# x and the first adaLN weights requested at once, small vectors by GpSimd, the first adaLN chain ahead of the casts, half of the spilt x written later

## The chip, the core and the metric

One core of a Trainium2 chip runs the whole kernel. The metric is device time in microseconds. Engines are named as in the profile: PE (TensorE), DVE (VectorE), ACT (ScalarE), POOL (GpSimd) and SP (SyncE, which here only issues DMAs). SP's transfers run on queue q1, POOL's on queue q0; the same 16 DMA engines serve both.

## The reference

One layer of a conditioned decoder trunk, for 256 prompt tokens and 8 x 8 sample tokens (320 rows in all) that share the weights. Only the start matters here:

```python
mod = jax.nn.silu(c) @ w_ada + b_ada                 # 9 conditioning rows, 2048 -> 6 x 2048
sh1, sc1, g1, sh2, sc2, g2 = jnp.split(mod, 6, axis=-1)
h = _rmsnorm(x, norm1_g) * (1 + sc1) + sh1
p = h @ w_in                                         # 2048 -> 11280: q, k, v, og, u, ga, gb, alr
...                                                  # linear attention, pooling, w_o, SwiGLU FFN
x = x + g1 * (merged @ w_o)                          # x is needed again here
```

## The kernel before

Activations lie transposed: 16 k-tiles of 128 channels x 320 tokens. Every projection splits weight and activation into a high and a low part and runs three matmuls for each pair of tiles (`mm3`, lines 171 to 173: `hh`x`whi`, `hl`x`whi`, `hh`x`wlo`). A weight chunk is loaded by SP into one of three `raw` buffers (line 149); ACT makes `whi` (line 157) and DVE makes `wlo` (line 158). The raw buffer is free for the next request once both have read it.

An adaLN block of 256 output channels is `hada`: `hada_load` fetches 2 MB of `w_ada` in two DMAs of 1 MB (lines 223 to 225; two `araw` buffers), 32 small matmuls use them (line 236), ACT copies the result out of PSUM (line 239), PE transposes it, and DVE reduces it, adds the bias and for section 1 folds in `norm1_g` (lines 244 to 249). Sections 0 and 1 (shift and scale) of the first two k-tiles are needed before any projection can start.

The head (lines 423 to 471) loads c, the small vectors and x. c lands in rows of `junk`, is transposed on PE (16 transposes, line 435), goes through silu into `scT`, and is then overwritten: `junk` also takes the output of the squares that give each row's norm (line 462). `h_pre(k)` (line 476) transposes x into `xT`, scales it with `rx` into `xh` and writes `xT` to a scratch in HBM (`xspill`, by POOL, line 484); the `w_o` stage reads it back. `h_post(k)` applies scale and shift (`affine`, lines 342 to 344) and splits the result into `hh[k]` and `hl[k]` (lines 337 and 338).

The projections of group 0 run in six slices of the contraction, `SLICES = ((0, 2), (2, 4), (4, 6), (6, 8), (8, 12), (12, 16))`. Each slice goes through seven units: q, k, u (256 columns each, one half unit) and v, og, ga, gb (512 columns each). Between units the adaLN blocks and `h_pre`/`h_post` of the next slice are emitted. The framework orders the instructions of each engine by a simulated timeline; `tc.high_priority` moves code ahead, `tc.issue_after(x)` holds an instruction behind another one of its engine. After slice 6 the kernel goes on with groups 1 to 3, `w_o`, and the FFN.

Of the kernel before, what the change touches and what calls it, by code (L numbers as in the profile page):

```python
# [79 lines left out]
def body(tc, A):  # L80
# [71 lines left out]
    def split(raw):  # L152
        n = raw.shape[2]
        hi = wp.tile([P, 512 // n, n], F32R, tag="whi", bufs=WB, name=nm("whi"))
        lo = wp.tile([P, 512 // n, n], F32R, tag="wlo", bufs=WB, name=nm("wlo"))
        hi, lo = hi[:, 0:raw.shape[1]], lo[:, 0:raw.shape[1]]
        S.copy(hi, raw)  # L157
        V.tensor_sub(lo, raw, hi.bitcast(F32))  # L158
        return hi, lo

# [59 lines left out]
    def hada_load(sec, b0, pool, eng):  # L220

        blk = sec * KT + b0
        t = pool.tile([P, KT, 2 * P], F32, tag="araw", bufs=2, name=nm("hraw"))
        for k in range(0, KT, 8):
            eng.dma_start(t[:, k:k + 8], wada[:, k:k + 8, blk * P:(blk + 2) * P])
        return t

    def hada(sec, b0, t, pool):
# [10 lines left out]
        S.copy(sb, ps[:, 0:w])  # L239
# [8 lines left out]
        if sec == 1:  # L248
            V.scalar_tensor_tensor(dst, dst, 1.0, N1G[:, b0:b0 + 2].unsqueeze(2).broadcast_to([P, 2, 9]),
                                   op0=ALU.add, op1=ALU.mult)  # L250

# [88 lines left out]
    def affine(x, a, b, kt):  # L340

        V.tensor_scalar(x[:, 0:TP], x[:, 0:TP], modp(a, kt), modp(b, kt), op0=ALU.mult, op1=ALU.add)
        V.tensor_tensor(s3(x[:, TP:T]), s3(x[:, TP:T]), mods(a, kt), op=ALU.mult)
        V.tensor_tensor(s3(x[:, TP:T]), s3(x[:, TP:T]), mods(b, kt), op=ALU.add)
# [78 lines left out]
    with tc.tile_pool(name="head", bufs=1) as xp:  # L423
        junk = xp.tile([P, D], F32, name="junk")
        crow = junk[0:9, :]
        nc.sync.dma_start(crow[0:1, :], A["c_prompt"])
        nc.sync.dma_start(crow[1:9, :], A["c_sample"])
# [13 lines left out]
        nc.sync.dma_start(vr0, A["b_ada"].rearrange("o (r p) -> (o r) p", p=P))  # L441
        vr1 = xp.tile([4 * KT + 4, P], F32, name="vr1")
        for j, n in enumerate(("norm1_g", "norm2_g", "final_norm_g", "pool_scale")):
            a = A[n] if n == "final_norm_g" else A[n][0]
            nc.sync.dma_start(vr1[16 * j:16 * j + 16, :], a.rearrange("(r p) -> r p", p=P))
        nc.sync.dma_start(vr1[64:68, :], A["gla_norm_g"][0].rearrange("(r p) -> r p", p=P))
        nc.sync.dma_start(xn[0], x2d[0:P])
        nc.sync.dma_start(xn[1], x2d[P:2 * P])
        nc.sync.dma_start(xn[2][0:TS], A["x_sample"].rearrange("b t d -> (b t) d"))
        raws = {(s, 0): hada_load(s, 0, xp, nc.sync) for s in (0, 1)}  # L450
# [9 lines left out]
        for i in range(3):  # L460
# [13 lines left out]
        spilt = []  # L474

        def h_pre(k):
# [3 lines left out]
            xT = xp.tile([P, T], F32, tag="xT", bufs=2, name=nm("xT"))  # L480
            xh = xhs[k] = xp.tile([P, T], F32, tag="xh", bufs=4, name=nm("xh"))
            S.copy(xT, pt[:, 0:T])
            V.tensor_tensor(xh, pt[:, 0:T], rx, op=ALU.mult)
            spilt.append(nc.gpsimd.dma_start(xspill[k], xT).ins)

        def h_post(k):
            xh = xhs.pop(k)
            affine(xh, 1, 0, k)
            hilo(hh[k], hl[k], xh)

# [21 lines left out]
        def h_rows(b):  # L512

            def load(s):
                raws[s, b] = hada_load(s, b, xp, nc.gpsimd)
# [6 lines left out]
        with tc.high_priority():  # L522
            h_rows(0)[4]()
        us = [u for u in units(0) if u[0] in "qku"] + [u for u in units(0) if u[0] not in "qku" and u[1] == 0]
        apool = [xp]
        for si, (k0, k1) in enumerate(SLICES):
            last = k1 == KT
            bg = [] if last else [f for b in range(*SLICES[si + 1], 2) for f in h_rows(b)]
            if last:
                with tc.issue_after(spilt[-1]):  # L530
# [7 lines left out]
            for ui, (kind, i, col) in enumerate(us):  # L538
# [607 lines left out]
```

## Time and profile before

| | us |
|---|---|
| median of 3 runs (1978.18 to 1979.74) | 1978.41 |
| the profiled execution | 1972.99 |
| its span in the profile | 1971.2 |
| PE busy in the span | 1924.5 |
| granted TensorE clock, mean share of full speed | 0.993 |

The span counts from the first instruction to the last; 1.8 us of the execution lie around it. The profiled execution is 5.4 us below the median of the timed runs. Times in the rows are from the start of the span.

### The profile page before, as it was taken

To read this page: it belongs to the slowest core of one execution; us is meant where nothing else is said; L and a number is where in the kernel's file an instruction comes from. 1 tells how busy PE (TensorE), PEld (TensorE's weight loads), DVE (VectorE), ACT (ScalarE), POOL (GpSimd) and SP (SyncE) were. 2 spreads that over 40 slices of the span, in tenths; PEclk is the share of its full clock that TensorE was granted. 3 is DMA by queue.
4 is the path that set the end of the run, shared out by engine and by line. 5 is a ranking of instruction groups with operands and counts; after the bars stand their busy time and mean duration, and the time that the engine had idled before them with its cause. 6 is when DMAs were issued, how large, how long until landed. Compare 5 with 4: busy or idle time off the path is not lost.

```text
span 1971.2 us, 34613 instructions
## 1 busy us (share of the span) xinstructions
PE 1924.5 (98%) x13808; PEld 1825.2 (93%) x13808; DVE 1007.0 (51%) x1935; ACT 826.9 (42%) x1485; POOL 207.3 (11%) x323
## 2 busy tenths in 40 slices
PE   5999999999999999999999999999999999999997
PEld 4889888988998899989989999999999999999997
DVE  3776454666355535665574444444444444444554
ACT  4433343544345433553354333333333434344443
POOL 2231131221121112111030000000000000000000
PEclk9999989999999999999999999999999999999998
DMA  9996647777875788579845555444545444444442
GB/s 349 354 354 237 203 150 264 219 230 251 256 223 188 247 268 272 183 249 321 269 153 158 186 188 182 145 150 144 156 145 155 150 150 150 150 151 144 149 139 98
DMA packets 287308, 400.60 MB, mean 203 GB/s; under 512 B 11953, under 2 KB 243921, under 8 KB 286809
## 3 DMA queue, kind: packets, MB, share of 16 engines
q1 hardware_dynamic: 250170, 261.81, 42.7%
q0 software_dynamic: 36976, 136.57, 19.5%
q8 instruction: 108, 1.77, 0.4%
q14 instruction: 54, 0.44, 0.1%
HBM read 373.90 MB, written 24.67 MB: 202 GB/s over the span
## 4 chain that ended last, share of the span: by engine, by line
PE 82%; DMA 3%; ACT 1%; DVE 0%; issue 0%; POOL 0%; ACTq 0%; DVEq 0%
PE ps L172 25%; PE ps L171 25%; PE ps L173 25%; PE pm L301 3%; PE pm L135 1%; DMA araw<-w_ada 1%; PE pm L786 1%; PE pm L807 1%; DMA raw<-w_o 1%; DMA S<-state_gla 1%; PE pm L752 1%; DMA o_gs<-S 0%; PE pm L782 0%; PE pm L591 0%; PE pm L741 0%; PE psy L171 0%
## 5 line engine op out<-in xcount | busy, mean ns | idle before, releaser
L158 DVE TENSOR_TENSOR wlo<-raw,whi 128x512 fp32r<-128x512 f32 x952 | 657.7, 694 | 792.4 <-ACT whi L157 779.9
L157 ACT CAST whi<-raw 128x512 fp32r<-128x512 f32 x952 | 587.8, 622 | 948.3 <-PE ps L172 830.1
L171 PE MATMUL ps<-hh,whi 128*128 128x320 f32 x1408 | 441.9, 314 | 6.1 <-ACT hh L337 2.6
L172 PE MATMUL ps<-hl,whi 128*128 128x320 f32 x1408 | 440.4, 313 | 0.0
L173 PE MATMUL ps<-hh,wlo 128*128 128x320 f32 x1408 | 437.4, 312 | 0.0
L172 PE MATMUL ps<-h2l,whi 128*128 128x320 f32 x1408 | 434.7, 309 | 0.0
L171 PE MATMUL ps<-h2h,whi 128*128 128x320 f32 x1408 | 434.7, 309 | 0.0
L173 PE MATMUL ps<-h2h,wlo 128*128 128x320 f32 x1408 | 434.2, 309 | 0.0
L171 PEld LDWEIGHTS ps<-hh,whi 128*128 128x128 f32 x1408 | 265.2, 188 | 19.7 <-issue 9.0
L172 PEld LDWEIGHTS ps<-hl,whi 128*128 128x128 f32 x1408 | 265.3, 188 | 10.4 <-issue 9.4
L173 PEld LDWEIGHTS ps<-hh,wlo 128*128 128x128 f32 x1408 | 264.7, 188 | 8.0 <-issue 5.3
L171 PEld LDWEIGHTS ps<-h2h,whi 128*128 128x128 f32 x1408 | 264.4, 188 | 3.4 <-ACT ah L337 3.4
L172 PEld LDWEIGHTS ps<-h2l,whi 128*128 128x128 f32 x1408 | 264.5, 188 | 0.1
L173 PEld LDWEIGHTS ps<-h2h,wlo 128*128 128x128 f32 x1408 | 264.5, 188 | 0.0
L171 PE MATMUL ps<-ah,whi 128*128 128x320 f32 x704 | 217.7, 309 | 0.0
L172 PE MATMUL ps<-al,whi 128*128 128x320 f32 x704 | 216.5, 308 | 0.0
L173 PE MATMUL ps<-ah,wlo 128*128 128x320 f32 x704 | 216.5, 308 | 0.0
L172 PEld LDWEIGHTS ps<-al,whi 128*128 128x128 f32 x704 | 132.0, 187 | 0.0
L171 PEld LDWEIGHTS ps<-ah,whi 128*128 128x128 f32 x704 | 131.9, 187 | 0.0
L173 PEld LDWEIGHTS ps<-ah,wlo 128*128 128x128 f32 x704 | 131.9, 187 | 0.0
L269 POOL DMA_DIRECT2D araw<-w_ada x64 | 55.1, 864 | 397.2 <-PE pm L301 385.9
L172 PE MATMUL ps<-ml,whi 128*128 128x320 f32 x256 | 79.3, 310 | 0.0
(282 smaller groups left out, 1634.2 us busy)
## 6 DMA issues: line engine op xcount, KB each, us to landing
raw<-w_gu SPq DMA_DIRECT2D x176, 512.0 KB, 3.5
raw<-w_in SPq DMA_DIRECT2D x170, 512.0 KB, 4.4
araw<-w_ada POOLq DMA_DIRECT2D x64, 1024.0 KB, 8.7
raw<-w_down SPq DMA_DIRECT2D x80, 512.0 KB, 3.5
hraw<-w_ada POOLq DMA_DIRECT2D x28, 1024.0 KB, 9.8
S<-state_gla POOLq DMA_DIRECT2D x16, 1024.0 KB, 8.3
o_gs<-S POOLq DMA_DIRECT2D x16, 1024.0 KB, 6.9
raw<-w_o SPq DMA_DIRECT2D x32, 512.0 KB, 6.2
```

Of the source, the lines that this page charges most:

```text
L135: PE.transpose(out, in_, ident[:k, :k])
L157: S.copy(hi, raw)
L158: V.tensor_sub(lo, raw, hi.bitcast(F32))
L171: PE.matmul(ps, lhsT=whi, rhs=xhi, start=start, stop=False)
L172: PE.matmul(ps, lhsT=whi, rhs=xlo, start=False, stop=False)
L173: last_mm[:] = [PE.matmul(ps, lhsT=wlo, rhs=xhi, start=False, stop=stop).ins]
L269: nc.gpsimd.dma_start(t[:, r:r + step], wada[:, k0 + r:k0 + r + step, col:col + nb * P])
L301: PE.matmul(ps[32 * j:32 * j + 32, 0:w], lhsT=scT[:, k0 + r + j, :], rhs=ada_raw[n][:, r + j, :], start=k0 == 0 and first, stop=k0 + nk == ...
L752: PE.matmul(pt, lhsT=E["kdn"][:, s, d * P:(d + 1) * P], rhs=E["vn"][:, s], start=s == 0, stop=s == 1)
L786: PE.matmul(pt[32 * j:32 * j + 32, :], lhsT=qeP[:, d, 4 * gg + j, :], rhs=E["S0", gg, d][:, j], start=False, stop=d == 0, tile_position=(0 ...
L807: PE.matmul(pt, lhsT=E["kpn"][:, j, d * P:(d + 1) * P], rhs=E["vp"][:, gg], start=True, stop=True)
```

## The change

- SP requests x first: the sample rows, then the two prompt tiles, then the four 1 MB pieces of `w_ada` for the first block of sections 0 and 1. For block 0 the upper half of the contraction (k-tiles 8 to 15), which the matmuls use first, is requested first.
- c, `b_ada` and the norm vectors are requested by POOL instead of SP; the identity matrix that the transposes need is made ahead of everything on POOL, and the zeroing of the unused rows of x moves from POOL to DVE.
- The first casts of weights (`whi` of q, k and u) may issue on ACT only after the copy of section 1's block; the first `wlo`, and the scaling of the next tiles, may issue on DVE only after `affine` of k-tile 0; `h_post(1)` follows it.
- POOL requests `w_ada` for the second block (`(s, b) == (0, 2)`) only after it has read the finished scale of block 0 (`anchor`). The matmuls of the second block are held behind the og unit of slice 1 (`first_mm`).
- For k below 8, `xT` lies in parts of the `merged` tiles that are not used yet, and its write to `xspill` is issued in the last slice, ahead of POOL's loads there.

```diff
-        S.copy(hi, raw)
-        V.tensor_sub(lo, raw, hi.bitcast(F32))
+        with tc.issue_after(first_casts[0]) if first_casts else nullcontext():
+            S.copy(hi, raw)
+        with tc.issue_after(first_casts[1]) if first_casts else nullcontext():
+            V.tensor_sub(lo, raw, hi.bitcast(F32))
...
-        for k in range(0, KT, 8):
+        for k in (8, 0) if b0 == 0 else (0, 8):
...
-        with tc.high_priority():
+        with tc.high_priority(), tc.issue_after(first_mm[0]) if first_mm else nullcontext():
...
+        with tc.high_priority():
+            make_identity(nc, ident)
+        nc.gpsimd.dma_start(crow[0:1, :], A["c_prompt"])
+        nc.gpsimd.dma_start(crow[1:9, :], A["c_sample"])
         xn = [xp.tile([P, D], F32, name="xn%d" % i) for i in range(3)]
-        G.memset(xn[2][TS:P], 0.0)
         x2d = A["x_prompt"][0]
+        nc.sync.dma_start(xn[2][0:TS], A["x_sample"].rearrange("b t d -> (b t) d"))
+        nc.sync.dma_start(xn[0], x2d[0:P])
+        nc.sync.dma_start(xn[1], x2d[P:2 * P])
+        raws = {(s, 0): hada_load(s, 0, xp, nc.sync) for s in (0, 1)}
         V.memset(scT, 0.0)
-        make_identity(nc, ident)
+        V.memset(xn[2][TS:P], 0.0)
...
-        for i in range(3):
+        for i in (2, 0, 1):
             n = P if i < 2 else TS
             S.activation(junk[:n], xn[i][:n], AF.Square, accum_out=ssq[:n, i:i + 1])
...
-            xT = xp.tile([P, T], F32, tag="xT", bufs=2, name=nm("xT"))
+            xT = merged[1 + k // 4 * 2][:, k % 4] if k < 8 else xp.tile([P, T], F32, tag="xT", bufs=2, name=nm("xT"))
             xh = xhs[k] = xp.tile([P, T], F32, tag="xh", bufs=4, name=nm("xh"))
             S.copy(xT, pt[:, 0:T])
-            V.tensor_tensor(xh, pt[:, 0:T], rx, op=ALU.mult)
-            spilt.append(nc.gpsimd.dma_start(xspill[k], xT).ins)
+            with tc.issue_after(first_casts[1]) if first_casts else nullcontext():
+                V.tensor_tensor(xh, pt[:, 0:T], rx, op=ALU.mult)
+            if k < 8:
+                parked.append((k, xT))
+            else:
+                spilt.append(nc.gpsimd.dma_start(xspill[k], xT).ins)
...
             def load(s):
-                raws[s, b] = hada_load(s, b, xp, nc.gpsimd)
+                with tc.issue_after(anchor(mod[:, KT, 0:1])) if (s, b) == (0, 2) else nullcontext():
+                    raws[s, b] = hada_load(s, b, xp, nc.gpsimd)
...
         with tc.high_priority():
-            h_rows(0)[4]()
+            evicted = hada(1, 0, raws.pop((1, 0)), xp)
+            first_casts += [evicted, h_post(0)]
+            with tc.issue_after(first_casts[1]):
+                h_post(1)
...
             if last:
+                with tc.issue_after(spilt[-1]):
+                    for k, xT in parked:
+                        nc.gpsimd.dma_start(xspill[k], xT)
...
+                if ui in (2, 4):
+                    first_mm[:] = last_mm if si == 0 else []
+                if ui == 2:
+                    first_casts.clear()
```

## Rows read from the trace of the kernel before

**Rows 1.** Windows: stretch, length, each engine's busy time (instructions), clock, DMA share, GB/s.

```profile
40.00:60.00 20.00, 20.00 (x182) 17.40 (x186) 11.85 (x31) 10.78 (x20) 4.68 (x6) 1.00 0.99 366
1000.00:1900.00 900.00, 899.34 (x6161) 886.44 (x6160) 423.82 (x711) 363.97 (x616) 20.09 (x40) 1.00 0.50 155
```

**Rows 2.** Timeline of PE: start, length, instruction, [idle before it <- what ended that].

```profile
3.86 1.84 PE L135 MATMUL pm<-cst,junk 9*128 9x9 f32 x16 [3.86 <-DMA junk<-c_sample]
...
24.84 1.93 PE L236 MATMUL pm<-hraw,scT 128*32 128x256 f32 x32 [0.42 <-DMA hraw<-w_ada]
28.62 0.44 PE L135 MATMUL pm<-cst,adasb 128*128 128x128 f32 x2 [1.84 <-ACT adasb L239]
...
32.27 0.90 PE L171 MATMUL ps<-hh,whi 128*128 128x320 f32 x2 [2.56 <-ACT hh L337]
...
35.93 1.93 PE L236 MATMUL pm<-hraw,scT 128*32 128x256 f32 x32
...
41.84 0.31 PE L171 MATMUL ps<-hh,whi 128*128 128x320 f32 x1
```

**Rows 3.** Timeline of SP's queue: when each request was issued.

```profile
0.74 0.35 SPq L426 DMA_DIRECT2D junk<-c_prompt  x1
...
4.08 0.35 SPq L447 DMA_DIRECT2D xn<-x_prompt  x1
...
5.58 11.27 SPq L225 DMA_DIRECT2D hraw<-w_ada  x4
...
27.31 1.38 SPq L149 DMA_DIRECT2D raw<-w_in  x2
```

**Rows 4.** Timeline of ACT in the head and the first units.

```profile
14.26 1.91 ACT L462 ACTIVATE junk<-xn 64x2048 f32<-64x2048 f32 x1 [0.40 <-DMA xn<-x_sample]
...
28.20 0.36 ACT L239 COPY adasb<-pm 128x256 f32<-128x256 f32 x1
...
31.76 0.82 ACT L337 CAST hh<-xh 128x320 fp32r<-128x320 f32 x2 [1.58 <-DVE xh L344]
35.95 0.62 ACT L157 CAST whi<-raw 128x512 fp32r<-128x512 f32 x1 [3.38 <-DMA raw<-w_in]
```

**Rows 5.** Timeline of DVE: scaling of x, first wlo, and the chain behind section 1.

```profile
22.09 0.89 DVE L483 TENSOR_TENSOR xh<-pm,rx 128x320 f32<-128x320 f32 x2
...
26.59 0.69 DVE L158 TENSOR_TENSOR wlo<-raw,whi 128x512 fp32r<-128x512 f32 x1 [1.68 <-ACT whi L157]
...
29.09 0.23 DVE L244 TENSOR_REDUCE mod<-pm 128x18 f32<-128x72 f32 x1
...
29.79 0.41 DVE L342 TENSOR_SCALAR xh<-xh,mod 128x256 f32<-128x256 f32 x1
```

**Rows 6.** Timeline of POOL: the requests for the second block's first section.

```profile
23.82 1.79 POOL L225 DMA_DIRECT2D hraw<-w_ada  x2 [1.82 <-PE pm L236]
```

**Rows 7.** Single raw requests, at 27.31, 29.05 and 170.27: KB, us to landing.

```profile
raw<-w_in SPq DMA_DIRECT2D x1, 512.0 KB, 8.6
...
raw<-w_in SPq DMA_DIRECT2D x1, 512.0 KB, 14.6
...
raw<-w_in SPq DMA_DIRECT2D x1, 512.0 KB, 3.6
```

**Rows 8.** PE's longest wait behind the head (timeline); windows around both long waits.

```profile
264.46 0.63 PE L171 MATMUL psy<-dh,whi 128*128 128x320 f32 x1 [2.42 <-ACT dh L337]
...
24.00:32.00 8.00, 3.45 (x42) 2.17 (x42) 5.15 (x16) 3.12 (x7) 4.55 (x6) 1.00 1.05 404
...
32.00:35.00 3.00, 2.73 (x10) 2.71 (x11) 0.89 (x2) 0.58 (x2) 0.00 (x0) 0.50 1.03 409
...
265.00:274.00 9.00, 7.67 (x27) 7.00 (x27) 2.64 (x6) 1.24 (x2) 2.37 (x6) 0.50 0.32 92
```

**Rows 9.** The last slice: POOL's first adaLN load (timeline), and its matmuls (one line's instructions).

```profile
149.12 1.80 POOL L269 DMA_DIRECT2D araw<-w_ada  x2 [2.63 <-DMA hraw<-w_ada]
...
L301 PE MATMUL pm<-araw,scT x128: 379/379/403, 209.6 to 246.7; 128*32 128x256 f32 x128
```

More of the change, by code (lines that the diff above doesn't have):

```diff
@@ L156, in split @@
         hi, lo = hi[:, 0:raw.shape[1]], lo[:, 0:raw.shape[1]]
-        S.copy(hi, raw)
-        V.tensor_sub(lo, raw, hi.bitcast(F32))
+        with tc.issue_after(first_casts[0]) if first_casts else nullcontext():
+            S.copy(hi, raw)
+        with tc.issue_after(first_casts[1]) if first_casts else nullcontext():
+            V.tensor_sub(lo, raw, hi.bitcast(F32))
         return hi, lo
+    first_casts = []
+    first_mm = []
     def split_chunk(src, nk, nn):
@@ L238, in hada @@
         sb = pool.tile([P, w], F32, tag="adasb", name=nm("adasb"))
-        S.copy(sb, ps[:, 0:w])
+        out = S.copy(sb, ps[:, 0:w]).ins
         pt = misc()
@@ L250, in hada @@
                                    op0=ALU.add, op1=ALU.mult)
+        return out
     PLAN = [(sec, b, 2, 16) for sec in (4, 2, 3) for b in range(0, KT, 2)] + [(5, 0, 4, 16), (5, 4, 4, 16), (5, 8, 4, 8), (5, 12, 4, 8)]
@@ L343, in affine @@
         V.tensor_tensor(s3(x[:, TP:T]), s3(x[:, TP:T]), mods(a, kt), op=ALU.mult)
-        V.tensor_tensor(s3(x[:, TP:T]), s3(x[:, TP:T]), mods(b, kt), op=ALU.add)
+        return V.tensor_tensor(s3(x[:, TP:T]), s3(x[:, TP:T]), mods(b, kt), op=ALU.add).ins
     xspill = dp.tile([KT, P, T], F32, name="xspill")
@@ L440, in body @@
         vr0 = xp.tile([6 * KT, P], F32, name="vr0")
-        nc.sync.dma_start(vr0, A["b_ada"].rearrange("o (r p) -> (o r) p", p=P))
+        nc.gpsimd.dma_start(vr0, A["b_ada"].rearrange("o (r p) -> (o r) p", p=P))
         vr1 = xp.tile([4 * KT + 4, P], F32, name="vr1")
@@ L444, in body @@
             a = A[n] if n == "final_norm_g" else A[n][0]
[L445 to L450, printed above, removed]
+            nc.gpsimd.dma_start(vr1[16 * j:16 * j + 16, :], a.rearrange("(r p) -> r p", p=P))
+        nc.gpsimd.dma_start(vr1[64:68, :], A["gla_norm_g"][0].rearrange("(r p) -> r p", p=P))
         pt = misc()
@@ L474, in body @@
         spilt = []
+        parked = []
         def h_pre(k):
@@ L479, in h_pre @@
                 tr(pt[:, i * P:(i + 1) * P], xn[i][:, k * P:(k + 1) * P])
-            xT = xp.tile([P, T], F32, tag="xT", bufs=2, name=nm("xT"))
+            xT = merged[1 + k // 4 * 2][:, k % 4] if k < 8 else xp.tile([P, T], F32, tag="xT", bufs=2, name=nm("xT"))
             xh = xhs[k] = xp.tile([P, T], F32, tag="xh", bufs=4, name=nm("xh"))
             S.copy(xT, pt[:, 0:T])
-            V.tensor_tensor(xh, pt[:, 0:T], rx, op=ALU.mult)
-            spilt.append(nc.gpsimd.dma_start(xspill[k], xT).ins)
+            with tc.issue_after(first_casts[1]) if first_casts else nullcontext():
[4 more added lines that the diff above has]
+                spilt.append(nc.gpsimd.dma_start(xspill[k], xT).ins)
         def h_post(k):
             xh = xhs.pop(k)
-            affine(xh, 1, 0, k)
+            done = affine(xh, 1, 0, k)
             hilo(hh[k], hl[k], xh)
+            return done
         def alr_proj(walr, cum):
```

2 lines of the change are left out of this document (removed).

## The prediction, made before the changed kernel ran

> **What bounds the kernel now.** I read the windows first. From 40 us on PE is busy without a gap, and so it is through the long stages [rows 1]. Whatever starts PE's dense work earlier therefore shortens the run by as much, unless PE later waits for what used to be in time. The timeline of PE shows where the dense work starts: the first projection matmul at 32.27, after a wait for `hh` [rows 2]. So the case is decided in the first 45 us, and I followed the chain that ends at 32.27 back through the timelines of PE, DVE, ACT and SP.
>
> The reader is to see three pieces. First, data: the last piece of `w_ada` for section 1 came at about 24.8, since PE stood ready and was released by that DMA [rows 2]. SP asked for x only at 4.08, behind seven small transfers, and for `w_ada` from 5.58 [rows 3]; between the two ends the queue simply works through its bytes. Second, the 32 matmuls of section 1, 1.93 us, ending at 26.77 [rows 2]. Third, 5.5 us from there to 32.27. That part is longer than its work: ACT was casting weights and copied the block only at 28.20, 1.43 us late [rows 4], and DVE put other tiles between the steps.
>
> **The request order.** SP's first request goes out at 0.74, its first for x at 4.08 [rows 3]. With the small ones gone, x goes out 3.34 us earlier, and all behind it on the same queue. I move the landing of the last piece from 24.8 to 21.5. The small vectors (about 150 KB) still need the same DMA engines; at the 366 GB/s of a busy stretch that is 0.4 us [rows 1], which the old order paid too.
>
> **The half order.** The upper half of each block is now first, and the matmuls use it first. In section 1 only 16 of 32 matmuls then stand behind the last landing: half of 1.93 is 0.97 us, a gain of 0.97. They end at 22.5.
>
> **The chain ahead of the casts.** Without foreign work I add its steps. Copy to transpose 0.42 (28.20 to 28.62), transpose to reduce 0.47 (to 29.09), reduce, bias and gain 0.70 (to 29.79), `affine` of one tile 0.8 (its first of three steps is 0.41, the others I estimate at half of that), cast of `hh` to first matmul 0.51 (31.76 to 32.27) and 0.1 for the first hand-over: 3.0 us [rows 2, 4, 5]. The first projection matmul so comes at 25.5, 6.8 us earlier than now: 3.3 from the requests, 1.0 from the half order, 2.5 from the chain.
>
> **What the wait of the casts costs.** The held `whi` casts are three of 0.62 us on ACT [rows 4]; they fit into the 2.6 us that the chain spends on PE and DVE behind the copy, so I take nothing. The held `wlo` is on the path of something else. Today the first `wlo` ends at 27.28, 5 us ahead of the first projection matmul, and frees a raw buffer; SP asks for v's weights at 27.31 [rows 3, 5]. After the change the first `wlo` runs only when `affine` of tile 0 is done, at about 25.0, and ends at 25.7. v's request thus moves 1.6 us earlier, while PE moves 6.8 us earlier. Queued behind it on DVE are `hl`, tile 1 and the next `wlo`; on SP the requests of og and ga.
>
> How long v then takes is the one large unknown. Three rows bound it: 8.6 us where POOL had its big loads out, 14.6 for the request two places behind, 3.6 with the engines free [rows 7]. At 25.7 POOL's first piece has been out for 1.3 us, against 3.5 us in the old case (23.82 to 27.31) [rows 3, 6], so the backlog is smaller but the competition is the same. I take 7.6, nearer to 8.6, and keep 5.8 to 8.6 for the forecast. v lands at 33.3, its cast takes 0.62 [rows 4], and v's matmuls start at 34.0.
>
> PE meanwhile has q, k and u: 36 matmuls. In the old run v started at 41.84, with one adaLN block (1.93) and its transposes (0.44) done in between [rows 2]; without these it is 39.5, so q, k and u took 7.2 us from 32.27. From 25.5 they end at 32.7. PE waits 1.3 us for v, where it used to have the second block as filler; that block is now held behind og, and its request by `anchor` until 24.3. **The sum** at this point is 39.5 less 34.0, 5.5 us earlier. og comes 0.3 us late by the same competition (its request waits for the second `wlo`): 5.2 us remain. With v at its bounds, landing 5.8 or 8.6 us after its request, they are 6.8 (PE then never waits) and 4.2.
>
> **The spill.** Eight writes of 160 KB, 1.3 MB, leave the first stages, worth some 3 us of DMA time there. No row before shows PE waiting for it, so I book no gain; it covers the idle stretch of the DMA engines between the first loads and POOL's held request. The eight requests now stand on POOL ahead of the last slice's loads: two of the larger ones took 1.79 us [rows 6], so eight take at most 7.2. The loads at 149.12 then issue up to 7 us later, and their matmuls start at 209.6 [rows 9]: a cover of 60 us. I take zero, up to 0.5 if q1's chunks are slowed for these 3 us.
>
> **Small moves.** The zeroing of x's unused rows took POOL 1.8 us; on DVE it lies in a stretch where DVE has nothing to do. c goes through POOL now. In the old run it was asked for at 0.74 and there at 3.86, and its transposes took 1.84 [rows 2, 3]. POOL makes the identity first and needs up to 0.9 us for each request [rows 6], so it has asked by about 3; I allow 4 us with x on the same engines, and c is there at 7. Since `junk` is reused, the squares wait for them. From the last square's start at 14.26 to scaled x at 22.09 it took 7.8 us [rows 4, 5]; three squares in a row add 4.2. Transposes, silu (0.3) and this put scaled x at about 21, 3 us before the scale of block 0 is. Zero cost.
>
> Here a rule speaks against the change. The Trainium skill (SBUF — State Buffer, "SBUF: two separate sides") says that a DMA issued by POOL has its descriptors written by GpSimd, which is locked out while VectorE runs a two-port operation, and advises SP or ACT instead. No run here shows such a lock. If the 1.9 us zeroing on DVE were such an operation, c would come at 9, still a us inside the cover, and the sum would not change.
>
> **The clock.** In the wait of 2.56 us before 32.27 the granted clock fell to half and stayed there past 35; after a wait of 2.42 us at 264 it was half until 274; the wait of 1.84 us before 28.62 left it whole [rows 2, 8]. Half is 1.2 GHz of 2.4. A fall of some 3.4 us costs 1.7 us of work, one of 10.2 us 5.1. My new wait before the first projection is about 2.0 us, and the one for v 1.3. If the clock holds at 25.5, q, k and u end sooner, and PE only waits longer for v, whose landing is fixed; so this changes the sum only when v is early. The Trainium skill (TensorE: Matmul & The Clock Gate, Part 1) adds that the monitor runs free of the kernel, so that the point of change shifts between runs; by that, either wait may fall on either side.
>
> **The rivals.**
>
> *No new wait.* v lands within 5.5 us and the clock holds at the start. For it: the queue is nearly empty when v is asked for. Against: 8.6 and 14.6 us in that stretch [rows 7]. Then 6.8 and half of the 1.7 us of half clock are kept: 7.6, or 1970.8.
>
> *Given back to the clock.* v lands 8.6 us after its request, PE waits 2.3 us, close to the 2.42 of the later fall, and the clock falls. For it: the row of v itself, and PE has lost its filler. With v at 8.6 the 4.2 us left lose 1.7 to 5.1 us: 1975.9 to 1979.3, no change to be seen.
>
> *Slower.* v is served like the third request of the old run, 14.6 us [rows 7], because POOL now puts four pieces out in one go ahead of it. Then v starts at 40.9, 1.4 us later than the old 39.5, plus a fall of 5.1: 6.5 us slower, 1985. With such a fall the change is slower than before once v takes over 8.6 us, and by 4 us once it takes over 11.7.
>
> *The head is bound elsewhere.* The change does not do what it says if c by POOL is late. c at 15 instead of 7 would put scaled x at 29 and the first projection at about 30.5: 1.8 us gained, no change to be seen. For it: the 14.6 us of a request in a full queue. Against it: c is only nine rows, and no more than x stands ahead.
>
> **How the numbers follow.** Forecast 52%, no new wait 14%, given back to the clock 19%, late c 5%, slower 10%. The profiled execution was 1972.99 for a span of 1971.2; the sum gives it 1967.8. Against the median of 1978.41 it is 1978.4 less 5.2, 1973.2; I carry the difference over, since nothing in the sum depends on where the 5.4 us between profile and median come from. A difference under 0.2%, 4 us, can't be told from none with this kernel. The forecast alone spans 1971.6 to 1974.2. The range reaches from the middle of the best rival, 1970.8, to the top of the clock's, 1979.3, and leaves out the slower case. Faster: forecast (less 4% in which the framework's new order loses a us elsewhere) and no new wait, 62%. Same: these 4, the clock and late c, 28%. Slower: 10%.
>
> **What would show it.** In the changed profile: SP's x requests at 0.7 to 2; section 1's last matmuls near 22; the copy right behind them; the first projection matmul at 25 to 26; v's `whi` cast released by its DMA at 32 to 34.5; no half clock after that; the loads of the last slice 5 us later without a wait for them. The forecast is wrong if the first projection matmul is not before 28, if PE waits over 2.4 us for v, or if waits show up in a stage that was dense before.

## The result and the profile after

The changed kernel is slower. Its median is 1984.3 us (1978.18 to 1991.05, 20 runs) against 1975.66 us (1970.51 to 1979.74, 20 runs) of the kernel before on the same chips: a ratio of 1.0046, 95% interval 1.0037 to 1.0056, or 9 us. The prediction was 5.2 us faster. (The three runs behind its 1978.41 are the three slowest of these 20.) The profiled execution took 1982.23 us, its span is 1980.1 us, its mean granted clock 0.994. (The new line numbers are up to 12 higher in the head and more behind it: `mm3` is now L176 to L178, the adaLN matmuls L241, `wlo` L160, `hl` L344.)

The windows of the changed kernel, with the columns of [rows 1]: stretch, length, busy time of PE, PEld, DVE, ACT and POOL, clock, DMA share, GB/s.

```profile
33.00:40.00 7.00, 4.70 (x17) 4.30 (x18) 3.48 (x8) 0.46 (x1) 2.93 (x4) 0.51 0.84 285
40.00:43.40 3.40, 1.31 (x9) 1.05 (x8) 0.91 (x2) 1.56 (x3) 0.00 (x0) 1.00 1.03 361
43.40:46.80 3.40, 3.17 (x12) 3.17 (x13) 0.38 (x1) 1.31 (x3) 0.00 (x0) 0.50 1.03 357
...
40.00:60.00 20.00, 17.68 (x132) 15.83 (x135) 7.69 (x13) 9.51 (x16) 1.75 (x2) 0.91 0.82 275
60.00:80.00 20.00, 16.77 (x170) 12.98 (x161) 11.94 (x30) 6.33 (x14) 3.51 (x4) 1.00 1.02 350
```

Between 40 and 60 us PE was busy for all of 20.00 us before [rows 1]; now it is 17.68, and 16.77 in the next 20 us. The clock is at half twice, for some 10.2 us together (before: once, for 3.4 us). PE's timeline shows where it waits; the last row is the counterpart of the long wait in [rows 8].

```profile
9.85 1.84 PE L135 MATMUL pm<-cst,junk 9*128 9x9 f32 x16 [9.85 <-DMA junk<-c_sample]
...
22.97 0.32 PE L135 MATMUL pm<-cst,vr 68*128 68x68 f32 x1
23.76 3.18 PE L241 MATMUL pm<-hraw,scT 128*32 128x256 f32 x32 [0.47 <-DVE rx L478]
...
27.71 1.93 PE L241 MATMUL pm<-hraw,scT 128*32 128x256 f32 x32
...
32.99 0.76 PE L176 MATMUL ps<-hh,whi 128*128 128x320 f32 x2 [1.47 <-ACT hh L343]
36.05 0.63 PE L177 MATMUL ps<-hl,whi 128*128 128x320 f32 x1 [2.30 <-DVE hl L344]
...
43.63 0.64 PE L176 MATMUL ps<-hh,whi 128*128 128x320 f32 x1 [2.32 <-ACT q L403]
...
69.27 1.93 PE L241 MATMUL pm<-hraw,scT 128*32 128x256 f32 x32 [2.73 <-DMA hraw<-w_ada]
...
274.76 0.42 PE L176 MATMUL psy<-dh,whi 128*128 128x320 f32 x1 [2.42 <-ACT dh L343]
```

At the last row the changed kernel is 10.3 us behind (274.76 against 264.46 [rows 8]). At the end of the span it is 8.9: the half clock behind that wait is 3.4 us long instead of 10.2, and small later waits take part of this back. So the loss lies where the gain was expected. It has these pieces: the first projection matmul comes at 32.99 instead of 25.5 as predicted, 0.7 us later than before; then PE waits 2.30 us for `hl`, 2.32 us for v and 2.73 us for a block of `w_ada`; and at the half clock PE is busy for 7.9 us (4.70 and 3.17 in the windows above), where before it was some 3.1 (2.73 in the 3 us of [rows 8], the rest just behind), 4.8 more, which costs half of that, 2.4. They sum to 10.5 us, close to the 10.3, though not exactly the same thing. The windows from the first projection matmul to the start of the long wait, before and then changed, give it in full:

```profile
32.27:262.04 229.77, 225.90 (x1852) 201.95 (x1852) 140.64 (x295) 86.23 (x166) 50.91 (x72) 0.99 0.82 290
32.99:272.34 239.35, 229.31 (x1852) 203.79 (x1852) 143.15 (x301) 86.21 (x166) 55.78 (x80) 0.98 0.86 289
```

Both have the same 1852 matmuls. PE is idle for 10.0 us instead of 3.9 and busy for 3.4 us more; with the later start that is 0.7 + 6.2 + 3.4 = 10.3. The three waits named are 7.35 of the 10.0; the smaller waits, which the first sum leaves out, were 1.2 us longer in the kernel before, and the busy time grew by 1.0 us more than the 2.4 worked out for the clock.

What released these waits stands in the timelines of the other engines, here in order of time.

```profile
1.31 0.65 POOL L434 DMA_DIRECT2D junk<-c_prompt  x1 [0.37 <-issue]
1.96 0.55 POOL L435 DMA_DIRECT2D junk<-c_sample  x1
...
2.47 13.14 SPq L230 DMA_DIRECT2D hraw<-w_ada  x4
...
30.00 0.37 ACT L244 COPY adasb<-pm 128x256 f32<-128x256 f32 x1 [2.61 <-PE pm L135]
...
32.35 3.58 POOL L230 DMA_DIRECT2D hraw<-w_ada  x4 [0.30 <-issue]
32.77 1.28 DVE L160 TENSOR_TENSOR wlo<-raw,whi 128x512 fp32r<-128x512 f32 x2
33.48 2.41 SPq L149 DMA_DIRECT2D raw<-w_in  x3
33.98 0.88 DVE L492 TENSOR_TENSOR xh<-pm,rx 128x320 f32<-128x320 f32 x2
34.78 0.68 DVE L160 TENSOR_TENSOR wlo<-raw,whi 128x512 fp32r<-128x512 f32 x1
...
35.51 1.10 DVE L344 TENSOR_TENSOR hl<-xh,hh 128x320 fp32r<-128x320 f32 x2
...
41.84 1.14 ACT L158 CAST whi<-raw 128x512 fp32r<-128x512 f32 x2 [5.76 <-DMA raw<-w_in]
...
56.50 1.75 POOL L230 DMA_DIRECT2D hraw<-w_ada  x2 [20.57 <-PE pm L241]
```

`w_ada` is asked for at 2.47 instead of 5.58 [rows 3], but its data are not much earlier. The head is the place to look at the DMA queues: from 14 to 24 us nothing but `w_ada` moves, in packets of 1 KB. First the kernel before, then the changed one (packets, MB, and the time of the packets as a share of 16 engines).

```profile
DMA packets 3819, 3.86 MB, mean 386 GB/s; under 512 B 49, under 2 KB 3819, under 8 KB 3819
...
q1 hardware_dynamic: 3819, 3.86, 108.7%
```

```profile
DMA packets 3468, 3.48 MB, mean 348 GB/s; under 512 B 69, under 2 KB 3468, under 8 KB 3468
...
q1 hardware_dynamic: 3468, 3.48, 109.1%
```

16 engines x 10 us x 1.087 / 3819 is 45.5 ns for a packet before, and 50.3 ns after; the median of the single packets is 46 and 51. The same transfer runs a tenth slower, with the engines as full in both. Nothing in the diff says that it should.

### The profile page after: what moved, and what is told of

Same layout as the page of the kernel before. It is cut to its first block, busy times and chain, and to the rows that moved or that the text cites. A ratio compares the mean times of both kernels' runs of the same rounds, so it can differ in the third digit from the quotient of the medians.

```text
span 1980.1 us, 34612 instructions
## 1 busy us (share of the span) xinstructions
PE 1926.2 (97%) x13808; PEld 1824.3 (92%) x13808; DVE 1008.0 (51%) x1936; ACT 826.1 (42%) x1485; POOL 212.4 (11%) x331
## 3 DMA queue, kind: packets, MB, share of 16 engines
q1 hardware_dynamic: 249904, 261.65, 42.5%
## 4 chain that ended last, share of the span: by engine, by line
PE 83%; DMA 1%; ACT 1%; POOL 0%; DVE 0%; issue 0%; ACTq 0%; DVEq 0%
PE ps L176 25%; PE ps L177 25%; PE ps L178 25%; PE pm L307 3%; PE pm L135 1%; PE pm L810 1%; PE pm L831 1%; PE pm L776 1%; DMA raw<-w_o 1%; DMA araw<-w_ada 1%; PE pm L765 0%; PE pm L806 0%; PE pm L706 0%; PE pm L615 0%; POOL w L890 0%; PE pm L787 0%
## 5 line engine op out<-in xcount | busy, mean ns | idle before, releaser
L160 DVE TENSOR_TENSOR wlo<-raw,whi 128x512 fp32r<-128x512 f32 x952 | 656.7, 693 | 788.1 <-ACT whi L158 775.6
L176 PE MATMUL ps<-hh,whi 128*128 128x320 f32 x1408 | 442.6, 315 | 6.2 <-ACT q L403 2.3
L178 PE MATMUL ps<-hh,wlo 128*128 128x320 f32 x1408 | 438.6, 313 | 0.1
L176 PE MATMUL ps<-h2h,whi 128*128 128x320 f32 x1408 | 434.6, 309 | 0.0
L178 PE MATMUL ps<-h2h,wlo 128*128 128x320 f32 x1408 | 434.1, 308 | 0.0
L176 PEld LDWEIGHTS ps<-hh,whi 128*128 128x128 f32 x1408 | 265.7, 189 | 21.4 <-issue 9.2
L178 PEld LDWEIGHTS ps<-hh,wlo 128*128 128x128 f32 x1408 | 265.5, 189 | 8.2 <-issue 5.3
L176 PEld LDWEIGHTS ps<-h2h,whi 128*128 128x128 f32 x1408 | 264.3, 188 | 3.4 <-ACT ah L343 3.4
L178 PEld LDWEIGHTS ps<-h2h,wlo 128*128 128x128 f32 x1408 | 264.4, 188 | 0.0
L176 PE MATMUL ps<-ah,whi 128*128 128x320 f32 x704 | 217.7, 309 | 0.0
L178 PE MATMUL ps<-ah,wlo 128*128 128x320 f32 x704 | 216.5, 308 | 0.0
L176 PEld LDWEIGHTS ps<-ah,whi 128*128 128x128 f32 x704 | 131.9, 187 | 0.0
L178 PEld LDWEIGHTS ps<-ah,wlo 128*128 128x128 f32 x704 | 131.9, 187 | 0.0
```

The lines of the kernel that those rows point to most:

```text
L176: PE.matmul(ps, lhsT=whi, rhs=xhi, start=start, stop=False)
L178: last_mm[:] = [PE.matmul(ps, lhsT=wlo, rhs=xhi, start=False, stop=stop).ins]
```

## The experiments

The traces gave three suspects on the engines' queues (theory A): c by POOL comes late; the held `wlo`, once released, goes ahead of `hl` on DVE and delays v's request; the second block, held behind og, no longer fills PE's wait for v and keeps its buffers until 56. The rival (theory B) was the slow packets. All timed comparisons are listed first (e0 and e8, single runs, stand in the text); "place" is where the `hraw` buffers begin in SBUF by the program's allocation, as the rest after division by 128.

| run | place | c late | wlo held | block held | ratio to before | interval |
|---|---|---|---|---|---|---|
| before | 0 | | | | 1 | |
| changed | 64 | x | x | x | 1.0046 | 1.0037 to 1.0056 |
| e1 | 64 | | x | x | 1.0028 | 1.0018 to 1.0039 |
| e2 | 64 | x | | x | 1.0021 | 1.0009 to 1.0033 |
| e3 | 64 | x | x | | 1.0011 | 1.0000 to 1.0022 |
| e7 | 64 | | | | 1.0014 | 1.0003 to 1.0025 |
| e6 (old half order) | 64 | x | x | x | 1.0051 | 1.0032 to 1.0071 |
| e9 (before, moved) | 64 | | | | 1.0026 | 1.0017 to 1.0036 |
| e10 | 0 | x | x | x | 1.0029 | 1.0016 to 1.0041 |
| e15 | 0 | x | x | | 0.9998 | 0.9987 to 1.0009 |
| e16 | 0 | | | x | 0.9991 | 0.9982 to 1.0000 |
| e11 | 0 | | | | 0.9998 | 0.9986 to 1.0009 |
| e12 (before, requests alone) | 0 | | | | 1.0002 | 0.9992 to 1.0013 |
| e4 (before, spill alone) | 0 | | | | 1.0002 | 0.9992 to 1.0011 |
| e13 (before, later buffers) | 0 | | | | 0.9990 | 0.9979 to 1.0001 |
| e14, e18 (e11, later buffers) | 0 | | | | 0.9982, 0.9984 | 0.9971 to 0.9994, 0.9974 to 0.9994 |
| e17 (later buffers) | 0 | | | x | 0.9996 | 0.9986 to 1.0007 |

### The three parts one at a time

e0 is the kernel before once more.

> The kernel before once more, unchanged, for a second trace. The trace of before moved w_ada at 386 GB/s between 14 and 24 us, that of the changed kernel at 348, with the same 1 KB pieces on the same queue. If the slower rate belongs to the change, this trace has 386 again; if it differs from execution to execution, it may have either.

It took 1976.58 us, with 386 GB/s from 14 to 24 us again. e1 asks for c by SP, ahead of x:

```diff
-        nc.gpsimd.dma_start(crow[0:1, :], A["c_prompt"])
-        nc.gpsimd.dma_start(crow[1:9, :], A["c_sample"])
+        nc.sync.dma_start(crow[0:1, :], A["c_prompt"])
+        nc.sync.dma_start(crow[1:9, :], A["c_sample"])
```

> The changed kernel, but c is requested first and by SP, as before the change. Theory 'late c' (the head is bound by the chain c, squares, scaled x): c is there near 4 instead of 9.8, the squares end with the last tile of x, near 15 instead of 18, and the first projection matmul comes 2 to 3 us earlier than 33.0; the time falls by 2 to 3 us from the changed kernel's. Rival 'landing' (the last piece of w_ada, 24.5, decides): the first projection stays within 1 us of 33 and the time too.

e2 lets `wlo` run as soon as its data are there:

```diff
-        with tc.issue_after(first_casts[1]) if first_casts else nullcontext():
-            V.tensor_sub(lo, raw, hi.bitcast(F32))
+        V.tensor_sub(lo, raw, hi.bitcast(F32))
```

> The changed kernel, but wlo is not held behind affine of tile 0. Theory 'held wlo' (the hold piles wlo, hl and the next tile up on DVE and sends v's request out late): the wait of 2.3 us for hl shrinks to under 1, v's weights are asked for 2 us earlier and the wait for them of 2.3 us goes; the time falls by 3 to 5 us. Rival 'second block' (PE waits for v because its filler is held): hl's wait shrinks, v's stays; 1 to 2 us.

e3 takes the hold from the second block's matmuls and the anchor from its request:

```diff
-                with tc.issue_after(anchor(mod[:, KT, 0:1])) if (s, b) == (0, 2) else nullcontext():
-                    raws[s, b] = hada_load(s, b, xp, nc.gpsimd)
+                raws[s, b] = hada_load(s, b, xp, nc.gpsimd)
...
-                    first_mm[:] = last_mm if si == 0 else []
+                    first_mm[:] = []
```

> The changed kernel, but the second adaLN block is neither held on PE nor its request on POOL. Theory 'second block': the block fills the wait for v, its buffers are free 15 us earlier, the wait of 2.7 us for w_ada at 69 goes; the time falls by 4 to 6 us. Theory 'held wlo': PE still waits for hl and v, only the wait at 69 goes; 2 to 3 us.

Each gives something back (3.6, 4.9 and 6.9 us of the 9; as differences of two ratios, each is uncertain by some 3 us, so their order is not shown). e1 is the most telling: its first projection matmul stands at 28.44, 4.5 us earlier than in the changed kernel, and this became 3.6 us of time, with waits of 2.55 us for `hl`, 1.68 for v and 2.45 for `w_ada` still there. e7 takes all three out.

> The changed kernel with three of its parts put back at once: c asked for by SP first, wlo not held, the second block and its request not held. Kept are the order of the large requests, the half order, the ACT casts held behind the first copy, and the parked spill. Theory A (three new waits cost the time: c's landing, the DVE order that puts wlo ahead of hl and delays v, the hold of the second block): first projection matmul at 28 to 29 us, v's matmuls without a wait, no wait at 62 to 70, and a time 3 to 6 us below the kernel before, near 1971. Theory B (the slower w_ada requests, 3.0 us per MB where the kernel before has 2.7, are the main loss): the time stays at or above the kernel before, 1975 to 1979, although no wait of over 1 us is left between 29 and 70 us.

1.0014, no better than e3 alone. By theory A it should have beaten the kernel before by 3 to 6 us; it is slower by 2.8. Its rate from 14 to 24 us is 348 GB/s, and PE waits 3.29 us for the second block at 42.5. The time is the one that theory B expected. Its condition, that no wait of over 1 us is left, is not met, so e7 makes the slow packets likely and does not show them to be the cause.

### What slows the packets

e6 puts the old half order back (`for k in range(0, KT, 8)`), e4 is the kernel before with the parked spill alone, and in e8 POOL asks for nothing in the head (c by SP first, the small vectors by SP behind `w_ada`).

> The changed kernel with the halves of each adaLN block in the old order, all else as changed. Theory A: the first projection waits for the chain of x and for PE's own queue, not for the last half, so the time is that of the changed kernel within 1 us (1984), and the rate of w_ada stays at 348 GB/s. Theory B: the half order makes the packets slower; the rate goes back to 386 GB/s, section 1's last piece lands about 2 us earlier, near 22.5, and the first projection matmul comes no more than 1 us earlier because the transposes of section 0 stand behind it. By the prediction's own step the old order would cost 0.97 us: 1985.

> The kernel before with the parked spill alone: eight of the writes of x go out behind the other spill instead of in the head. Theory A (the spill is hidden either way): same as before within 1 us, w_ada at 386 GB/s in the head, the loads of the last slice issued some 10 us later and PE never waiting for them. Theory B (the eight writes in the middle slow the loads of the next stage, or the freed DMA time in the head brings the weights earlier): a change of 2 us or more either way, with a new or a shorter wait on PE behind a DMA.

> The changed kernel with c asked for by SP first and the small vectors by SP behind w_ada, so that POOL asks for nothing in the head. It tells what slows the packets of w_ada. Theory A (POOL's small requests on the same DMA engines): w_ada moves at 386 GB/s again and section 1's last piece lands near 22. Theory B (the order of the large requests or of the halves): 348 GB/s as in the changed kernel, landing near 24.5. The small vectors come late and their transpose stands ahead of section 0's block on PE, so the first projection matmul is expected between 30 and 36 us, and the time near the changed kernel's.

e6 and e8 stay at 348 GB/s, so neither the half order nor POOL's requests are the cause. e4 has 381 GB/s (386 but for the first quarter of a us, in which x still moves), so it is not the parking. e4 also settles the spill: 1.0002, with the loads of the last slice issued from 148.40 on, and no wait of PE for them; 1.3 MB less in the first stages was worth nothing. e6 shows no effect of the half order (1985.6 against 1984.3), but its interval of 1.0032 to 1.0071 leaves room for some 3 us less and 5 us more. e8, a single run, took 1998.25 us: its vectors stand ahead of section 0's block on PE and came at 23.78.

What is left was in no line of the diff. The new call of `hada_load` stands ahead of three small tiles, so the allocation puts `hraw` 1600 bytes lower: at byte 133312 of each partition instead of 134912. 134912 is a multiple of 256; 133312 is 64 past a multiple of 128. e9 adds an unused tile of 64 bytes per partition to the kernel before, e10 the same tile to the changed kernel, e11 to e7:

```diff
+        pad = xp.tile([P, 16], F32, name="pad")
+        V.memset(pad, 0.0)
         raws = {(s, 0): hada_load(s, 0, xp, nc.sync) for s in (0, 1)}
```

> The kernel before with one unused tile of 64 bytes per partition allocated ahead of the buffers hraw, so that these (and the buffers of the last slice's blocks, araw, in the same place) begin at 134976, 64 bytes past a multiple of 128, where they began at 134912, a multiple of 256. Nothing else is changed. Theory A (the place of the destination in SBUF sets the packet time): a 1 KB packet of w_ada takes 51 ns instead of 46, the head loads at 348 GB/s instead of 386, POOL's 4 KB packets take 186 ns instead of 162, and the time is 3 to 6 us above the kernel before. Theory B (the order of the requests sets it): 386 GB/s and 162 ns as before, and the same time within 1 us.

> The changed kernel with the same unused tile of 64 bytes ahead of hraw: the buffers begin at 133376, a multiple of 256, where the change had put them at 133312, 64 bytes past a multiple of 128. Theory A (place): 386 GB/s, the last piece of section 1 at 22.3 instead of 24.5, POOL's 4 KB packets at 162 ns; the three waits of the change stay but get shorter, and the time lies 3 to 6 us under the changed kernel, so still 3 to 5 us over the kernel before. Theory B (order): no difference to the changed kernel, 1984.

> The run with three parts out (c by SP, wlo free, second block free) and the 64 bytes. Theory A: the waits are gone and so is the slow transfer; the second block lands 3 us earlier, near 39, first projection matmul near 28, time 2 to 5 us under the kernel before, near 1971 to 1974. Theory B: as without the 64 bytes, ratio 1.001 to the kernel before.

The DMA queues from 14 to 24 us, e9 and then e10:

```profile
DMA packets 3446, 3.48 MB, mean 348 GB/s; under 512 B 48, under 2 KB 3446, under 8 KB 3446
...
q1 hardware_dynamic: 3446, 3.48, 109.7%
```

```profile
DMA packets 3822, 3.82 MB, mean 382 GB/s; under 512 B 94, under 2 KB 3822, under 8 KB 3822
...
q1 hardware_dynamic: 3822, 3.82, 107.7%
```

Shifting `hraw` by 64 bytes turns its rate, both ways; the pairs differ otherwise only in the unused tile, its memset and the places of the small tiles behind it. Its price is known four times: 5.1 us in e9 against before (3.4 to 7.1 by its interval), 3.3 us between the changed kernel and e10, 3.2 us between e7 and e11, 2.6 us between e3 and e15 (below). The last three are differences of two ratios, uncertain by some 3 us each; only together with e9 do they say something of the size. PE's timeline of e9 shows how it reaches the time:

```profile
26.86 1.93 PE L236 MATMUL pm<-hraw,scT 128*32 128x256 f32 x32 [1.77 <-DMA hraw<-w_ada]
...
33.79 0.90 PE L171 MATMUL ps<-hh,whi 128*128 128x320 f32 x2 [2.56 <-ACT hh L337]
...
269.14 0.63 PE L171 MATMUL psy<-dh,whi 128*128 128x320 f32 x1 [2.43 <-ACT dh L337]
```

Section 1 starts 2.0 us later than in [rows 2], the first projection 1.5 us, and the long wait 4.7 us (264.46 in [rows 8]).

### The first step alone

e12 is the kernel before with the prediction's first step only: c, x and `w_ada` by SP at once, the small vectors by POOL, the zeroing on DVE, `hraw` at a multiple of 256.

```diff
         x2d = A["x_prompt"][0]
+        nc.sync.dma_start(xn[0], x2d[0:P])
+        nc.sync.dma_start(xn[1], x2d[P:2 * P])
+        nc.sync.dma_start(xn[2][0:TS], A["x_sample"].rearrange("b t d -> (b t) d"))
+        pad = xp.tile([P, 16], F32, name="pad")
+        V.memset(pad, 0.0)
+        raws = {(s, 0): hada_load(s, 0, xp, nc.sync) for s in (0, 1)}
...
-        nc.sync.dma_start(vr0, A["b_ada"].rearrange("o (r p) -> (o r) p", p=P))
+        nc.gpsimd.dma_start(vr0, A["b_ada"].rearrange("o (r p) -> (o r) p", p=P))
```

> The kernel before with the first step of the prediction alone: c by SP, then x and the first w_ada pieces at once, the small vectors by POOL, zeroing on DVE; the old order of halves, no held casts, no parked spill, hraw at a multiple of 256. The prediction's step: the last piece of section 1 lands 2.5 to 3.3 us earlier, near 22, and the first projection matmul comes as much earlier, at 29 to 30; 2.5 to 3.3 us under the kernel before. Rival: the transfers are the bound up to 50 us, not their start; then the earlier start is worth no more than the 2 us in which the DMA engines had been idle at the start, and v and the second block take the rest, 0 to 2 us under it.

```profile
30.25 0.56 PE L171 MATMUL ps<-hh,whi 128*128 128x320 f32 x2 [2.65 <-ACT hh L337]
...
264.69 0.42 PE L171 MATMUL psy<-dh,whi 128*128 128x320 f32 x1 [2.42 <-ACT dh L337]
```

The last piece of section 1 landed at 22.66, 2 us earlier than before, and the first projection starts 2.0 us earlier (32.27 in [rows 2]). At 264 nothing of it is left, and the time is the same: 1.0002. (Single traces of kernels that are alike up to that wait reach it at 264.46, at 265.40 in e0 and at 266.19 in e13 below, with a first half clock of 3.4, 6.8 and 6.8 us. Differences of under 2 us at this row are no finding by themselves.) The windows of e12 show where it goes:

```profile
100.00:120.00 20.00, 19.37 (x169) 16.62 (x168) 14.09 (x30) 6.37 (x13) 4.21 (x6) 1.00 0.89 333
120.00:140.00 20.00, 18.83 (x165) 16.12 (x164) 12.66 (x30) 6.54 (x14) 5.55 (x8) 1.00 0.96 354
```

In the kernel before PE is busy for 20.00 and 19.56 us in these two stretches. Up to 100 us e12 had done 1.7 us more of PE work; here it loses 1.4 of it, in waits of up to 0.7 us for DVE (`mod`, `og`, `wlo`). So the time is that of the rival of that run, but not by its reason, transfers that bound the start up to 50 us: PE kept the lead up to 100 us and then ran into a stretch that something else paces. What sets that pace I did not test; fewer bytes alone (e4) did not change the time.

### Which of the waits costs

With the packets at their old speed, e10 still takes 1.0029. e15 is e10 with the second block free, e16 is e10 with c by SP and `wlo` free, the block still held.

> The changed kernel with the 64 bytes ahead of hraw and without the hold of the second block and of its request; c by POOL and the held wlo stay. Theory A (the hold of the second block is the larger of the waits): the wait for w_ada near 66 is gone, PE has the block as filler when v is late, and the time is within 2 us of the kernel before, 1975 to 1977. Theory B (c by POOL and the order on DVE cost the most): the time stays near that of the changed kernel with the 64 bytes, 1979 to 1981.

> The counterpart: the changed kernel with the 64 bytes, c asked for by SP and wlo free, but the second block and its request still held. Theory A: the first projection matmul comes at 28, and the time is still 3 to 5 us over the kernel before, 1978 to 1980, with a wait of 2 to 3 us for w_ada between 55 and 65. Theory B: the time is that of the kernel before, 1975 to 1977.

Both theories fall by half: either half of the parts can stay. PE's timeline, first e10, then e15, then e16:

```profile
31.85 0.56 PE L176 MATMUL ps<-hh,whi 128*128 128x320 f32 x2 [1.47 <-ACT hh L343]
34.91 0.64 PE L177 MATMUL ps<-hl,whi 128*128 128x320 f32 x1 [2.50 <-DVE hl L344]
...
42.00 0.41 PE L176 MATMUL ps<-hh,whi 128*128 128x320 f32 x1 [2.31 <-ACT q L403]
...
66.68 1.93 PE L241 MATMUL pm<-hraw,scT 128*32 128x256 f32 x32 [2.43 <-DMA hraw<-w_ada]
...
270.22 0.63 PE L176 MATMUL psy<-dh,whi 128*128 128x320 f32 x1 [2.42 <-ACT dh L343]
```

```profile
32.16 0.56 PE L176 MATMUL ps<-hh,whi 128*128 128x320 f32 x2 [1.48 <-ACT hh L343]
...
35.20 3.54 PE L241 MATMUL pm<-hraw,scT 128*32 128x256 f32 x32 [2.47 <-DMA hraw<-w_ada]
...
266.20 0.41 PE L176 MATMUL psy<-dh,whi 128*128 128x320 f32 x1 [2.42 <-ACT dh L343]
```

```profile
31.93 0.90 PE L175 MATMUL ps<-hh,whi 128*128 128x320 f32 x2 [4.97 <-ACT hh L342]
...
263.08 0.54 PE L175 MATMUL psy<-dh,whi 128*128 128x320 f32 x1 [2.42 <-ACT dh L342]
```

The three start the first projection within 0.3 us of each other, and reach the long wait at 270.22, 266.20 and 263.08. In e15 the 2.5 us behind the first matmuls stay, now ended by the block's data; but the block then fills PE while v is on its way, and the waits for v and at 66 are gone. In e16 there is no filler, and none is needed. Its SP and POOL queues, and the request for v (KB, us to landing):

```profile
27.13 1.87 SPq L149 DMA_DIRECT2D raw<-w_in  x3
...
29.65 3.57 POOL L229 DMA_DIRECT2D hraw<-w_ada  x4 [0.24 <-issue]
```

```profile
raw<-w_in SPq DMA_DIRECT2D x1, 512.0 KB, 3.7
```

The free `wlo` lets SP ask for v 2.5 us ahead of POOL's 4 MB, and it lands after 3.7 us. In e10 it is asked for at 32.35, 1.1 us behind POOL's first piece (31.21), and takes 7.8. So the change's wait for v needs both: a held `wlo` that puts v behind POOL's pieces, and a held block that leaves PE nothing to do meanwhile. (e16 also has c by SP; e2 and e3, which free `wlo` alone and the block alone, have no wait for v either.) The wait at 66 goes with it: in e10 the held block runs at 52, POOL may refill its buffers at 54.23, and the next block is wanted at 64. In e16 the same hold ends 4 us earlier (block at 47.87, request at 50.13), in time.

### The later buffers

Some buffers of later stages also begin off a multiple of 128: the second pair of `raw` buffers and the `araw` behind them at 64, the `araw` of the long stages at 96. e13 moves them in the kernel before, e14 in e11, e17 in e16; e18 is e14 on another occasion.

```diff
     hp = hcx.enter_context(tc.tile_pool(name="hp", bufs=1, side="right"))
+    hpad = hp.tile([P, 24], F32, name="hpad")
+    nc.vector.memset(hpad, 0.0)
...
+    fpad = fp.tile([P, 16], F32, name="fpad")
+    nc.vector.memset(fpad, 0.0)
     fa = ctx.enter_context(tc.tile_pool(name="fa", bufs=1))
```

> The kernel before with unused tiles that move the load buffers of the later stages: araw of the long stages from 96 bytes past a multiple of 128 to a multiple (96 bytes), the second set of raw buffers and the araw behind them from 64 past to a multiple (64 bytes). The head is as before. If the place of the destination sets the packet time everywhere, POOL's 4 KB packets from 500 to 900 us take 160 to 165 ns instead of 175, and the waits of PE for araw near 475 and 675 (1 to 2 us) and for the adaLN blocks near 914 get shorter: 2 to 5 us under the kernel before, near 1971. If those stages have slack for their loads, the packets get faster and the time stays the same within 1 us.

> The three parts out, the 64 bytes ahead of hraw, and the later buffers moved too. It is the candidate to beat both kernels: the gain of the later buffers, if any, on top of a head whose earlier start has so far not reached the end; 1970 to 1975. If both the head and the later stages have slack, it equals the kernel before, 1975.

> The changed kernel with c by SP, wlo free, the hold of the second block kept, and all load buffers at multiples of 128: the run with only the hold (ratio 0.9991) and the moved later buffers (0.9990 alone) together. If the two add, 3 to 4 us under the kernel before, near 1971.5, the same as the candidate without the hold (0.9982). If v asked for ahead of POOL's pieces is worth more than the block as filler once the rest is in place, a further 1 to 2 us, 1970. If the gains of both sit in the same slack, 1974.

> The same program as the run with three parts out and all load buffers moved, on another occasion. If its ratio of 0.9982 is of the program, it comes out below 0.999 again, 1971 to 1972.5. If it was chance, since each of its neighbours lies between 0.999 and 0.9998, it comes out between 0.9990 and 1.0000, 1972.5 to 1974.5.

In e13 the median 4 KB packet from 900 to 1200 us went from 169 to 159 ns; from 500 to 900 us it stayed (174 and 173), so there the place was not what slowed it. A second part of the same run goes against the rule too: in the long stage the chunks of `w_gu` go to `raw` buffers at a multiple of 128 and to the second pair at 64 past it, by turns. In the kernel before, the median 1 KB packet is 46 ns in both, and a request lands after 3.5 us in both; e13, which moves the pair, has the same 46 ns and 3.5 us. The time of e13 is 2 us lower, at the edge of its interval (0.9979 to 1.0001). e14 and e18 are the same program on two occasions: 0.9982 and 0.9984, 3.6 and 3.2 us faster than before, both intervals below 1. This is the one version that beats both kernels, by less than the 0.2% that the prediction called its limit. e17, expected to be as good, has 0.9996; its interval (0.9986 to 1.0007) overlaps theirs, so that it is worse is not shown.

## Why the prediction was wrong

The sum failed at its first result and at its waits. The first projection matmul came 7.5 us later than the 25.5 of the sum, and 7.1 of these are there when section 1's matmuls end (29.64, not 22.5): the terms for the request order and for c and x. Then PE waited 2.30, 2.32 and 2.73 us where the sum had 1.3 and 0.3: the hold of `wlo` and the hold of the second block. Two of its own signs of being wrong came true: the first projection after 28, and waits in a stage that was dense. The wait for v stayed just under its limit of 2.4.

**What bounds the kernel.** That the case is decided by when PE's dense work starts and by later waits was right. That a start earlier by x is worth x was not: e12 starts 2.0 us earlier and ends at the same time, and e10 starts together with e15 and e16 and ends 6 and 7 us behind them. The clause "unless PE later waits" was there; the waits were not sized.

**The request order (3.3 us).** Wrong in size. The last piece landed at 24.53, not 21.5. The earlier request alone was worth 2.0 us (e12: 22.66, against 24.71 in the kernel before); why not 3.3 was not tested. Of these 2.0 the changed kernel kept 0.2, and the largest part of the rest went with the place of the destination, which the diff does not show: e10, same order, other place, has the piece at 23.13, 1.4 us earlier. The place was in no term and no bound of the range.

**c and x at zero cost.** Wrong. c was needed at 9.85, where I had 7, and the squares of x follow it. I took the cover of x's chain to be scaled x against the scale of block 0; but PE's queue runs in order, and section 0's block stands behind the transposes that wait for x. Its data had landed at 18.5, it began at 23.76, and it ran 3.18 us where the same 32 matmuls of section 1 took 1.93 (up to 26.3 its matmuls came at half the pace; the profile's clock row reads 1.00 there). I had named "late c" as a rival with 5%. e1 prices it: with c by SP the first projection comes 4.5 us earlier. The cover would have been too short even so: in e1 section 1's matmuls end at 24.6, not 22.5. The Trainium skill (SBUF — State Buffer, "SBUF: two separate sides"), cited in the prediction, says that GpSimd cannot write a DMA's descriptors while VectorE holds it out; by that the prediction had put c at 9. c_sample landed at 9.71, and the zeroing ran from 2.04 to 3.80. That fits, but no run here took the zeroing away alone, and x moved on the same engines, so the cause of the late c is open.

**The chain (3.0 us).** Right: from the copy at 30.00 to the first projection matmul at 32.99 it is 2.99 us. The copy came 0.36 us behind the end of section 1's matmuls (29.64) instead of 0.1: section 0's second transpose stood between them on PE, and ACT waited for it. The hold of `wlo` is what keeps the chain short: in e16, with `wlo` free, `wlo` runs inside it on DVE, and from the copy at 25.38 to the first projection matmul at 31.93 it is 6.55 us.

**The wait for v (1.3 us).** The mechanism was right, 8.3 us from request to landing where I took 7.6. The wait was 2.32 us, as in the rival that gives the gain back to the clock, and the clock fell. What I missed is on DVE: the hold released two `wlo`, two `xh` and a third `wlo` together, all of them ahead of `hl`, and PE waited 2.30 us for that, with the clock at half.

**og (0.3 us).** Wrong. I costed the hold of the second block by og's landing, and not by who waits for the block's buffers: POOL's next request went from 38.19 to 56.50, and PE waited 2.73 us at 69.

**The half order and the spill.** The half order had nothing to give, since neither block's matmuls waited for data in the changed kernel (23.76 and 27.71 in its PE timeline; e6 agrees, within its wide interval). The spill at zero was right in time (e4), though not in its bound: the loads of the last slice issue at 167.79 instead of 149.12, 18.7 us later and not up to 7, and PE still did not wait for them.

## What to carry to other kernels

A hold on one engine releases everything behind it at once: list what becomes ready together and in which order the engine takes it, and who waits for the buffers that the held work keeps. Two halves of a change (here c by POOL with the held `wlo`, and the held block) can each be free and cost 6 us together, so undo the parts singly and in groups. And when a load is moved in the code, look at where its buffer ends up: compare the packet times of the two traces before believing any theory about order.

## What the runs showed of the hardware

**The place of a DMA's destination.** The 1 KB packets of `w_ada` took 50.3 ns instead of 45.5, 348 GB/s instead of 386, when `hraw` began 64 bytes past a multiple of 128 and the engines moved nothing else for 10 us. The first `raw` buffers begin at 29824, 128 past a multiple of 256, and their 1 KB packets take 46 ns when they are alone, so there 128 is enough. But 64 past is not enough for a cost: `w_gu`'s 1 KB packets took 46 ns at such a place as at others (before against e13). One difference is that 512 of them took 2.1 us for a request, about 250 GB/s, so the engines were less full; that this is the condition is not tested. The Trainium skill (DMA: Bandwidth & Descriptors, "How a descriptor splits into AXI transactions") says that a transaction must start at a multiple of 256 B, so that a descriptor that begins elsewhere fetches unused bytes ahead of its start; it says so of reads. The runs show a cost for a destination in SBUF, of a tenth for `hraw`, and none at 128; whether it has the same reason is not shown.

**The clock behind the same wait.** The wait of 2.42 us that the kernel before has at 264 stands in every run. The half clock behind it lasted 10.24 us in the profiled execution of before, 3.41 us in e0, the same kernel, and it did not come at all in e3, e11 and e12. At half clock 10.24 us are 5.1 us of work, which a single execution can have or not, so two profiles must be compared ahead of that wait and not at their ends.
